# Moving the split normed activations to another byte phase in SBUF

## The chip, the cores and the metric

The kernel runs on one core of a Trainium2 chip. The metric is device time in microseconds of one execution; lower is better. SBUF is the on-chip memory in which the matmul operands lie, 128 partitions wide; an address below is a byte offset within a partition, and its phase is that offset modulo 256.

## The reference

A two-layer encoder trunk, float32, 256 tokens of width 1024. Each layer runs three sub-layers, each on a normed and modulated copy of the residual stream:

```python
n1 = modulate(rms_norm(h, norm_g[l, 0]), sh1, sc1)
h = h + 0.5 * g1[:, None, :] * swiglu(n1, ffn_wg[l, 0], ffn_wu[l, 0], ffn_wd[l, 0])
n2 = modulate(rms_norm(h, norm_g[l, 1]), sh2, sc2)
y = token_mixing(n2, ...)            # two attentions, gates, two output projections
h = h + g2[:, None, :] * y
n3 = modulate(rms_norm(h, norm_g[l, 2]), sh3, sc3)
h = h + 0.5 * g3[:, None, :] * swiglu(n3, ffn_wg[l, 1], ffn_wu[l, 1], ffn_wd[l, 1])
```

`swiglu` is `(silu(x @ w_gate) * (x @ w_up)) @ w_down` with an inner width of 2816. Shift, scale and gate come from a conditioning vector through a further 1024 x 9216 matrix per layer. A final RMS norm closes the stack.

## The kernel before

Every large product is made in three passes over split operands: each float32 operand is kept as a high part and a low part (`nh` and `nl` for the normed activations, `whi` and `wlo` for weights, `hh` and `hl` for the FFN's inner activations), both of type float32r, and `mm3` issues high x high (L84), low weights x high (L85) and high weights x low (L86). A matmul has a stationary operand, which a weight load (LDWEIGHTS, engine PEld) brings into the array, and a moving operand, which streams through it. In the trace's names `out<-moving,stationary`.

The six sub-layers (`SUBS`) run one after another. An FFN sub-layer (`ffn`) goes through eleven slices of 256 inner columns: `gate_up_mm` makes the slice's gate and up banks, 96 matmuls with `nh` or `nl` moving (256 tokens) and 128 weight columns stationary; `gate_up_act` makes `hh` and `hl`; `down_mm` then has `hh` or `hl` stationary and 512 weight columns moving. The first slice after a boundary is made token-major instead (`tok_hi`, `tok_lo`, L465 to L474): there `nh` or `nl` is stationary and the weights move. The mixer uses the token-major form for `pj` and `kv`, the other form for `pt` (`proj_T`) and for the gates `gt` (`gate_mm`); its merge (`yb`) and its output projection (`wo`) use slots of the weight pool on both sides. `gate_bcast` spreads a gate row over all partitions with the all-ones tile `onesr` stationary and `gh`, `gl` moving (L273, L274).

Weights come through one DMA queue (SP) into four raw buffers in the order of `stream`; `pump` takes the next half tile, casts it on ACT (L299), subtracts on DVE (L300), and asks for the next load when a raw buffer is done. The order on every engine is the program's order.

SBUF is laid out by pools, one after another in the order of their declaration (L45 to L47): `wp` (raw buffers of 8192 bytes and 23 slots of 4096), `op` (`nh`, `nl` of 8192 and three each of `hh`, `hl` of 2048), `sb` (everything else). Within a pool tags follow in order of first use. `wp` starts at 128 modulo 256 and all its and `op`'s tiles are multiples of 256 bytes, so weights, normed activations and FFN activations all lie at 128. `sb` starts at 128 too; its first tiles are `cb` (4096 bytes), eight buffers of 2048, `h0` and `h1` (4096 each), `ccol` (32), `abc` (384), `ngc` (192), `ident` (512) and then `onesr`.

`nh` and `nl` are made by `new_nT` (L395), one buffer each, and written by `mod_hi` (L377, ACT) and `mod_lo` (L392, DVE), in the first sub-layer by `mod_k` (L1142, L1145).

Of the kernel before, what the change touches and what calls it, by code (L numbers as in the profile page):

```python
# [13 lines left out]
F32 = mybir.dt.float32  # L14
F32R = mybir.dt.float32r
# [4 lines left out]
P = 128  # L20
D = 1024
S = 256
# [3 lines left out]
NK = D // P  # L26
# [15 lines left out]
def trunk(tc, a):  # L42
    nc = tc.nc
    with (
        tc.tile_pool(name="wp", bufs=1) as wp,  # L45
        tc.tile_pool(name="op", bufs=1) as op,
        tc.tile_pool(name="sb", bufs=1) as sb,  # L47
        tc.tile_pool(name="ps", bufs=1, space=bass.MemoryType.PSUM) as ps,

# [5 lines left out]
        def nm(s):  # L55
            uid[0] += 1
            return f"{s}_{uid[0]}"
# [7 lines left out]
        def b2(name, shape=(P, 512), dt=F32):  # L65
            return sb.tile(list(shape), dt, tag="b2", bufs=NB2, name=nm(name))
# [13 lines left out]
        def const(name, shape, dt=F32):  # L80
            return sb.tile(list(shape), dt, tag=name, bufs=1, name=name)
# [10 lines left out]
                              reason="order")  # L92


        cb = const("cb", [P, D])
        crow = [b2("crow", (1, D // 2)) for _ in range(2)]
        for hf in range(2):
# [13 lines left out]
        for hf in range(2):  # L111
            x = slice(hf * 512, (hf + 1) * 512)
# [280 lines left out]
                                            nh[:, kk, tok].bitcast(F32), op=ALU.subtract)  # L393

        def new_nT():  # L395
            return (op.tile([P, NK, S], F32R, tag="nh", bufs=1, name=nm("nh")),
                    op.tile([P, NK, S], F32R, tag="nl", bufs=1, name=nm("nl")))

        def residual(l, s, t, x, acc):
            g = mods[(l, s)]["g"]  # L400
# [782 lines left out]
        nc.scalar.dma_start(abc, a["ada_b_col"])  # L1183
        nc.scalar.dma_start(ngc, a["norm_g_col"])
        nT = new_nT()
        xsT = [slot("xsT", (P, 4, S)) for _ in range(2)]
        ns = [Norm(t) for t in range(2)]
# [16 lines left out]
        for i, (l, s) in enumerate(SUBS):  # L1204
            nxt = new_nT() if i + 1 < len(SUBS) else None
            if s == 1:
                norm1 = mixer(i, nT, norm1, consts, nxt)
            else:
                norm1, consts = ffn(i, nT, norm1, (lambda *x, nT=nT: first(nT, *x)) if i == 0 else None, nxt)
            nT = nxt  # L1210
# [78 lines left out]
```

## Time and profile before

| | us |
|---|---|
| median of 3 runs | 1146.72 (1146.51 to 1147.17) |
| the profiled execution, its own time | 1147.27 |
| its span, first to last instruction | 1145.5 |
| PE busy | 1122.6 |
| DVE busy | 868.5 |
| ACT busy | 587.7 |

Busy times of an engine are unions of its instructions' intervals. Matmuls are pipelined: the mean duration of one is longer than the step to the next start, so the step is read from start times and not from durations. The page's slices are 1/40 of the span each.

### The profile page before, as it was taken

What the parts mean: (1) busy time and instruction counts of PE and PEld (TensorE: products, weight loads), DVE (VectorE), ACT (ScalarE), POOL (GpSimd) and SP (SyncE); (2) the same over time, 40 slices, a digit from 0 to 9 for tenths busy, and PEclk for the clock granted to TensorE, in tenths of its full rate; (3) what the DMA queues carried; (4) which work ended last, traced back from release to release, by engine and by line L of the source; (5) the groups of instructions that cost most, each with busy time, mean ns of one, the idle gap of its engine ahead of it and who ended that gap; (6) DMA issues with size and microseconds to landing.
All of it is one profiled execution on the core that took longest, in us unless ns stands there. A gap on an engine that the chain in (4) does not pass through costs nothing.

```text
span 1145.5 us, 19136 instructions
## 1 busy us (share of the span) xinstructions
PE 1122.6 (98%) x7774; PEld 1037.2 (91%) x7774; DVE 868.5 (76%) x1334; ACT 587.7 (51%) x911; POOL 43.2 (4%) x52
## 2 busy tenths in 40 slices
PE   5999999999999999999999999999999999999997
PEld 3999999898899899999989999989889988999996
DVE  6996985899867798896489786469986778765543
ACT  4553474557665554445355445435766547544432
POOL 1000000130000000000000000004000100000000
PEclk9999999999999999999999999999999999999999
DMA  9997995368555388988439977543764454866500
GB/s 325 375 339 288 376 337 188 111 240 316 219 182 185 111 315 334 349 331 315 157 118 357 336 299 263 194 169 137 271 218 166 144 207 151 298 263 222 195 31 37
DMA packets 42584, 271.11 MB, mean 237 GB/s; under 512 B 5624, under 2 KB 6392, under 8 KB 12544
## 3 DMA queue, kind: packets, MB, share of 16 engines
q1 hardware_dynamic: 40036, 267.93, 63.7%
q10 hardware_dynamic: 2460, 1.96, 0.6%
q8 instruction: 61, 1.00, 0.3%
q14 instruction: 27, 0.22, 0.1%
HBM read 268.82 MB, written 1.05 MB: 236 GB/s over the span
## 4 chain that ended last, share of the span: by engine, by line
PE 94%; DVE 2%; issue 1%; DMA 1%; ACT 1%; POOL 0%; POOLq 0%; DVEq 0%; ACTq 0%
PE g L86 7%; PE u L86 7%; PE dn L84 7%; PE u L84 7%; PE dn L85 7%; PE u L85 7%; PE g L85 7%; PE g L84 7%; PE dn L86 7%; PE gt L84 3%; PE gt L86 3%; PE gt L85 3%; PE pt L85 1%; PE pt L84 1%; PE yb L84 1%
## 5 line engine op out<-in xcount | busy, mean ns | idle before, releaser
L300 DVE TENSOR_TENSOR wlo<-raw,whi 128x1024 fp32r<-128x1024 f32 x364 | 437.4, 1220 | 155.4 <-PE u L85 93.1
L299 ACT CAST whi<-raw 128x1024 fp32r<-128x1024 f32 x364 | 373.9, 1050 | 226.2 <-PE u L86 87.1
L84 PE MATMUL g<-nh,whi 128*128 128x256 f32 x656 | 186.5, 284 | 3.6 <-ACT nh L1142 3.6
L86 PE MATMUL g<-nl,whi 128*128 128x256 f32 x656 | 186.3, 284 | 1.6 <-DVE nl L1145 1.6
L84 PE MATMUL u<-nh,whi 128*128 128x256 f32 x656 | 186.3, 284 | 0.0
L85 PE MATMUL u<-nh,wlo 128*128 128x256 f32 x656 | 186.2, 284 | 0.0
L86 PE MATMUL u<-nl,whi 128*128 128x256 f32 x656 | 186.1, 284 | 0.0
L85 PE MATMUL g<-nh,wlo 128*128 128x256 f32 x656 | 186.1, 284 | 0.0
L84 PE MATMUL dn<-whi,hh 128*128 128x512 f32 (+1 forms) x358 | 138.7, 387 | 0.0
L85 PE MATMUL dn<-whi,hl 128*128 128x512 f32 (+1 forms) x358 | 138.4, 387 | 0.0
L86 PE MATMUL dn<-wlo,hh 128*128 128x512 f32 (+1 forms) x358 | 138.0, 386 | 0.0
L84 PEld LDWEIGHTS g<-nh,whi 128*128 128x128 f32 x656 | 126.4, 193 | 5.5 <-ACT nh L1142 4.0
L86 PEld LDWEIGHTS g<-nl,whi 128*128 128x128 f32 x656 | 126.2, 192 | 1.9 <-DVE nl L1145 1.9
L85 PEld LDWEIGHTS g<-nh,wlo 128*128 128x128 f32 x656 | 126.3, 193 | 1.3
L84 PEld LDWEIGHTS u<-nh,whi 128*128 128x128 f32 x656 | 126.6, 193 | 0.0
L86 PEld LDWEIGHTS u<-nl,whi 128*128 128x128 f32 x656 | 126.4, 193 | 0.1
L85 PEld LDWEIGHTS u<-nh,wlo 128*128 128x128 f32 x656 | 126.4, 193 | 0.0
L232 DVE CUSTOM_DVE_ANT_0 raw<-raw,cb 128x1024 f32<-128x1024 f32 x96 | 114.6, 1216 | 9.4 <-DMA raw<-in_ada_t_dram 9.4
L505 ACT ACTIVATE sg<-g 128x512 f32<-128x512 f32 x41 | 24.5, 597 | 109.7 <-PE g L86 109.5
L86 PEld LDWEIGHTS dn<-wlo,hh 128*128 128x128 f32 x358 | 67.3, 188 | 13.8
L84 PEld LDWEIGHTS dn<-whi,hh 128*128 128x128 f32 x358 | 67.4, 188 | 12.6
L85 PEld LDWEIGHTS dn<-whi,hl 128*128 128x128 f32 x358 | 67.4, 188 | 12.3
(202 smaller groups left out, 1895.4 us busy)
## 6 DMA issues: line engine op xcount, KB each, us to landing
raw<-in_w_gu_dram SPq DMA_DIRECT2D x79, 1024.0 KB, 5.9
raw<-in_w_d_dram SPq DMA_DIRECT2D x41, 1024.0 KB, 5.9
raw<-in_ada_t_dram SPq DMA_DIRECT2D x40, 1024.0 KB, 6.0
raw<-in_ada_g_dram SPq DMA_DIRECT2D x24, 1024.0 KB, 5.2
raw<-in_w_in_dram SPq DMA_DIRECT2D x16, 1024.0 KB, 4.9
raw<-in_w_gate_dram SPq DMA_DIRECT2D x16, 1024.0 KB, 4.9
raw<-in_w_gu_dram SPq DMA_DIRECT2D x18, 512.0 KB, 6.2
raw<-in_ada_t_dram SPq DMA_DIRECT2D x16, 512.0 KB, 6.9
```

Source lines behind the costliest of these rows:

```text
L84: nc.tensor.matmul(out, Lh, Rh, start=start, stop=False, skip_group_check=True)
L85: nc.tensor.matmul(out, Ll, Rh, start=False, stop=False, skip_group_check=True)
L86: nc.tensor.matmul(out, Lh, Rl, start=False, stop=stop, skip_group_check=True)
L232: queue("dve", nc.vector.tensor_tensor_reduce(r, r, cb, 1.0, 0.0, op0=ALU.mult, op1=ALU.add, accum_out=col[:, k:k + 1]))
L299: queue("act", nc.scalar.copy(hi, r))
L300: queue("dve", nc.vector.tensor_tensor(lo, r, hi.bitcast(F32), op=ALU.subtract))
L505: nc.scalar.activation(sg, g, AF.Silu)
```

## The change

A pool `mv` is declared between `op` and `sb`. Its first tile, `shift`, has 48 floats (192 bytes) per partition and is never used. `nh` and `nl` move from `op` to `mv`, behind it; they are declared flat, of the same size, and used through a view of the old shape. Thereby they start at 128 + 192 = 320, which is 64 modulo 256. The weights' pool and `hh`, `hl` stay at 128. `sb`, which comes after `mv`, starts 192 bytes later than before.

```diff
         tc.tile_pool(name="op", bufs=1) as op,
+        tc.tile_pool(name="mv", bufs=1) as mv_,
         tc.tile_pool(name="sb", bufs=1) as sb,
@@
+        mv_.tile([P, 48], F32, tag="shift", bufs=1, name="shift")
         cb = const("cb", [P, D])
@@
         def new_nT():
-            return (op.tile([P, NK, S], F32R, tag="nh", bufs=1, name=nm("nh")),
-                    op.tile([P, NK, S], F32R, tag="nl", bufs=1, name=nm("nl")))
+            return (mv_.tile([P, NK * S], F32R, tag="nh", bufs=1, name=nm("nh")).rearrange("p (k x) -> p k x", k=NK),
+                    mv_.tile([P, NK * S], F32R, tag="nl", bufs=1, name=nm("nl")).rearrange("p (k x) -> p k x", k=NK))
```

## Rows read from the trace of the kernel before

**Rows 1.** Page, engine totals (busy us, share, instructions) and granted clock by slice.
```profile
span 1145.5 us, 19136 instructions
PE 1122.6 (98%) x7774; PEld 1037.2 (91%) x7774; DVE 868.5 (76%) x1334; ACT 587.7 (51%) x911; POOL 43.2 (4%) x52
...
PEclk9999999999999999999999999999999999999999
```

**Rows 2.** Page, the chain that ended last, by engine.
```profile
PE 94%; DVE 2%; issue 1%; DMA 1%; ACT 1%; POOL 0%; POOLq 0%; DVEq 0%; ACTq 0%
```

**Rows 3.** Waits of PE, the longest: us in total, times, longest us.
```profile
PE nt L366 <- DVE xs L357: 7.9, 4, 6.5
```

**Rows 4.** Matmul groups by line and shape, xcount | busy us, mean ns | idle.
```profile
L84 PE MATMUL g<-nh,whi 128*128 128x256 f32 x656 | 186.5, 284 | 3.6 <-ACT nh L1142 3.6
L86 PE MATMUL u<-nl,whi 128*128 128x256 f32 x656 | 186.1, 284 | 0.0
...
L84 PE MATMUL dn<-whi,hh 128*128 128x512 f32 x346 | 135.3, 391 | 0.0
...
L86 PE MATMUL gt<-nl,whi 128*128 128x256 f32 x256 | 72.4, 283 | 0.0
...
L86 PE MATMUL pt<-nl,whi 128*128 128x256 f32 x128 | 36.4, 284 | 0.0
L465 PE MATMUL pj<-whi,nh 128*128 128x512 f32 x64 | 25.5, 399 | 0.0
...
L465 PE MATMUL gu<-whi,nh 128*128 128x512 f32 x48 | 18.7, 390 | 0.0
...
L793 PE MATMUL sc<-kaT,qaT 64*128 64x256 f32 x96 | 9.6, 300 | 0.1
...
L465 PE MATMUL kv<-whi,nh 128*128 128x256 f32 x32 | 7.9, 285 | 0.0
```

**Rows 5.** Timeline of PE (start us, duration us), a gate/up block's first start and the next.
```profile
104.01 0.28 PE L84 MATMUL g<-nh,whi 128*128 128x256 f32 x1
...
115.52 0.40 PE L84 MATMUL dn<-whi,hh 128*128 128x512 f32 x1
```

**Rows 6.** Timeline of PE, inside a down block and through the gate broadcast behind it.
```profile
152.00 0.39 PE L86 MATMUL dn<-wlo,hh 128*128 128x512 f32 x1
...
154.72 0.39 PE L86 MATMUL dn<-wlo,hh 128*128 128x512 f32 x1
154.95 0.39 PE L273 MATMUL gb<-gh,onesr 128*128 128x512 f32 x1
...
155.88 0.28 PE L84 MATMUL g<-nh,whi 128*128 128x256 f32 x1
```

**Rows 7.** Timeline of PE, from a down block into the next projection.
```profile
213.28 0.39 PE L465 MATMUL pj<-whi,nh 128*128 128x512 f32 x1
...
214.64 0.39 PE L465 MATMUL pj<-whi,nh 128*128 128x512 f32 x1
```

**Rows 8.** Timeline of PE, the merge after a gate broadcast.
```profile
346.48 0.28 PE L84 MATMUL yb<-oaH,whi 128*128 128x256 f32 x1
...
346.83 0.29 PE L84 MATMUL yb<-oaH,whi 128*128 128x256 f32 x1
346.96 0.28 PE L85 MATMUL yb<-oaH,wlo 128*128 128x256 f32 x1
...
357.99 0.40 PE L84 MATMUL wo<-whi,mT 128*128 128x512 f32 x1
```

**Rows 9.** ACT's split line: xcount, duration ns min/median/max, first and last start.
```profile
L299 ACT CAST whi<-raw x364: 1028/1050/1087, 15.2 to 1104.7; 128x1024 fp32r<-128x1024 f32 x182
```

**Rows 10.** Windows: PE, PEld, DVE, ACT, (POOL) busy; clock; DMA; first two: `nh`, `nl` alone.
```profile
0.00:87.00 87.00, 48.13 (x256) 41.87 (x257) 2.74 (x4) 4.37 (x8) 1.00 0.96 347
0.00:87.00 87.00, 36.71 (x128) 25.30 (x128) 2.74 (x4) 1.00 0.96 347
...
412.00:570.00 158.00, 158.00 (x1124) 149.29 (x1123) 122.72 (x144) 71.07 (x83) 0.95 (x1) 1.00 0.82 310
```

## The prediction

> **What bounds the kernel now.** [...] Then the chain of work that ended last [rows 2]: 94% of it is PE, spread over the three matmul lines of `mm3` (L84 to L86), which all stages share. Then who PE waited for [rows 3]: the longest of four items is 7.9 us in all. So the time is the number of matmuls times the step from one start to the next, plus little.
>
> A busy PE is not a PE at its peak, so the step is the next thing to read, from the start times. A gate/up block (8 k x 2 c x 2 banks x 3 = 96 matmuls of 256 moving columns) runs from 104.01 to 115.52 us [rows 5]: 11.51 us / 96 = 119.9 ns. Inside a down block the starts 152.00 and 154.72 are twelve matmuls of 512 columns apart [rows 6]: 2.72 / 12 = 226.7 ns. The difference, 106.8 ns for 256 more columns, is the column rate; both shapes then carry the same remainder, 119.9 - 106.8 = 13.1 ns. [...] This remainder is what the change can touch. It is large: over the 5,088 matmuls counted below, 13.1 ns each is 67 us.
>
> **The change, part by part.** (1) It adds one pool and one 192-byte tile that nobody writes or reads, and it writes the two normed tiles as flat tiles with a view. No instruction, DMA or semaphore wait is added or removed; the regions read and written by each instruction are the same, so the order on every queue stays, SP's and POOL's included. Cost: nothing, with no cover needed.
>
> (2) `nh` and `nl` move from 128 to 64 modulo 256 (128 + 192 = 320). They are the moving operand of gate/up, of the mixer's gates and of the transposed projections, with the weights at 128 as the stationary one. By [rows 4]: six groups of 656 (two are shown), three of 256 `gt`, three of 128 `pt`: 3936 + 768 + 384 = 5,088 matmuls of 256 columns. They are the stationary operand in the token-major products: three groups of 64 `pj` and three of 48 `gu`, 336 matmuls of 512 columns, and 96 `kv` of 256. Together 5,520 of PE's 7,774 [rows 1] get a stationary and a moving operand 64 bytes apart where both lay at the same phase. The 1,038 `dn` matmuls, in three groups (the shown form is 346 of each), and `yb` and `wo` keep equal phases.
>
> (3) The pool `sb` starts 192 bytes later. Its tiles keep their distances to each other; only the 96 narrow score matmuls [rows 4], a key in `sb` against a query in a slot, change phase. At 13.1 ns each that is 1.3 us either way, the bound of the side effect, and I take nothing.
>
> (4) The engines that write and read the moved tiles: the trace has no copy of one kind at two phases with the same operands, so what a phase costs ACT or DVE is bounded by the spread they show over many slots. The 364 casts of L299 take 1028 to 1087 ns [rows 9]. The instructions on `nh` and `nl` lie beside PE's work, which waits 7.9 us at most for anything of one kind [rows 3]. Nothing, within 1 us.
>
> So all hangs on one unknown: the step of a matmul whose two operands lie 64 bytes apart. The trace of before has no such pair in a long run. The bounds:
>
> Faster end: the remainder vanishes, -13.1 ns. Slower end: the nearest row with unequal phases. In `gate_bcast` the stationary `onesr` lies in `sb` behind `ident`, at 224 (128 + 32 + 384 + 192 + 512 bytes of tiles before it, modulo 256, the larger ones being multiples), and the moving `gh` and `gl` at 128. Four of them start at 154.95 and hand over at 155.88 [rows 6]: 0.93 / 4 = 232.5 ns, 5.8 ns more than the down step just before. That this is not the price of merely switching tiles shows at the hand-over from the down block to the next projection, both phases equal: 213.28 to 214.64 is six matmuls at 226.7 ns from the first one on [rows 7].
>
> Value taken: zero. Two readings speak for it. First, the mean step does not care how the streams lie against each other in time. After a gate broadcast the first 96 `yb` matmuls (two calls of `merge`) run unevenly: three starts to 346.83 and the next at 346.96 are 117 and 130 ns apart on average, yet 346.48 to 357.99 is 11.51 us again [rows 8], the same as the even block of [rows 5]. A cost set by where two readers meet in a 256-byte pattern ought to change when one is shifted by some ns against the other. Second, if placement within SBUF mattered by collision, ACT's and DVE's steady traffic at ever different slots should move either PE's step or their own times; the step stays at 119.9 and the casts within some 3% [rows 5, 9]. The broadcast is only four matmuls long, so its 5.8 ns may be the cost of a transient, and it starts 32 bytes off a multiple of 64, where the new place does not.
>
> [...]
>
> **The sum.** The profiled execution took 1147.27 us, 1.8 around its span; the median of the three runs is 1146.72, 0.55 less. Parts 1, 3, 4: 0. Part 2: 5,520 x 0. Forecast: 1146.7, with its own range 1144.5 to 1149 from the 1.3 us and 1 us above.
>
> **Rivals.** A, faster: equal phases are what the remainder is. For it: one and the same number of cycles once per weight load in both shapes, as when a weight load and a moving stream that start at the same phase keep each other up. Against it: the two readings above and the broadcast, which lies apart and is slower. Price: matmuls before 87 us gain nothing, since there the DMA engines are 96% busy at 347 GB/s [rows 10] and loads would end the waits; that is 256 + 128 = 384 of the 5,088. Left: 4,704. All of it gone: 4,704 x 13.1 = 61.6 us, 1085. Half gone, because the streams are a quarter of the pattern apart and not half: 30.8 us, 1116. Later stages can feed that: from 412 to 570 us DVE is busy 122.72 of 158 us, DMA 82% [rows 10], so 5% more demand fits, with some loss. I take 1116 for A.
>
> B, slower: unequal phases cost what the broadcast shows. For it: the only direct row. Place: the gate/up blocks, where nothing covers a longer step, since PE is the chain. Price: 5,520 x 5.8 ns = 32 us, 1179. If only half of it stays once the streams have settled, 1163. It decides from 2.3 us / 5,520 = 0.4 ns a matmul on, a third of a percent of the step.
>
> C: the change does not do what it says, because the allocator rounds the pool's start and the tiles keep one phase. Then 1146.7 too, and the trace after would look as in the likeliest case. I give it 0.02 within that case: 192 is a multiple of 32, as are the smallest tiles that already follow each other in `sb`.
>
> **How the numbers follow.** Same, C included: 0.42. A: 0.33, of which 0.12 below 1100. B: 0.25, of which 0.07 above 1179. Leaving out those two tails, 0.19, the range is 1100 to 1179. Faster, within, or slower by more than 0.2% (2.3 us, about what a measurement of this kernel tells from no change): 0.33, 0.42, 0.25. The likeliest gives the time.
>
> **What would show it.** In the profile of after: the 96 starts of a gate/up block again 11.5 us apart, and down blocks at 226.7 ns (they must stay there in every case, as their phases are kept). A: the gate/up block shrinks to 10.3 to 10.9 us, PE's waits on loads before 87 us grow. B: it grows to about 12 us. Wrong by another way: a new wait on `nh` or `nl` in who PE waited for, or ACT and DVE times on these tiles that differ by more than the spread above.

## The result, and the profile after

The changed kernel takes 1129.02 us, the median of four executions (1128.36 to 1130.47), against 1146.73 us before on the same chip: ratio 0.9847, 95% interval 0.983 to 0.9864, so 17.7 us or 1.5% faster. The profiled execution took 1128.88 us, its span is 1127.1.

The page of the changed kernel (engine totals as busy us, share, instructions; granted clock by slice; chain by engine):

```profile
span 1127.1 us, 19136 instructions
...
PE 1104.9 (98%) x7774; PEld 1019.7 (90%) x7774; DVE 867.4 (77%) x1334; ACT 588.4 (52%) x911; POOL 43.8 (4%) x52
...
PEclk9999999999999999999999999999999999999999
...
PE 91%; DVE 6%; issue 1%; DMA 1%; ACT 1%; POOL 1%; POOLq 0%; DVEq 0%
```

Against [rows 1] the instructions are the same, PE is busy 17.7 us less (1122.6 to 1104.9), and what it idles hardly changes (22.9 and 22.2 us). The chain [rows 2] names DVE for 6% now, but PE lost no time to it: no DVE wait has grown in the list of waits, whose longest item is this (columns: waiter, what it waited for, total us, times, longest us; before [rows 3]):

```profile
PE nt L369 <- DVE xs L360: 6.9, 2, 5.9
```

So the gain lies in the busy time itself, in the step from one matmul to the next. The matmul groups of the changed kernel (line, shape, count, busy us, mean ns), which answer to [rows 4]:

```profile
L85 PE MATMUL g<-nh,whi 128*128 128x256 f32 x656 | 185.0, 282 | 3.7 <-ACT nh L1145 3.7
...
L85 PE MATMUL dn<-whi,hh 128*128 128x512 f32 x346 | 135.1, 390 | 0.0
...
L87 PE MATMUL gt<-nl,whi 128*128 128x256 f32 x256 | 71.1, 278 | 0.0
...
L468 PE MATMUL pj<-whi,nh 128*128 128x512 f32 x64 | 25.6, 399 | 0.0
```

Durations overlap, so they hint only: `g` and `gt` are a little shorter, `dn` and `pj` are not. The start times tell. The timeline of PE after the change (start us, duration us), at the places of [rows 5 to 8]: a gate/up block, the down block behind it, the start of the next gate/up block; the gate broadcast; six steps of the next projection; 96 steps of the merge; a stretch of 85 gate/up matmuls at the end of a mixer:

```profile
101.15 0.28 PE L85 MATMUL g<-nh,whi 128*128 128x256 f32 x1
...
112.46 0.39 PE L85 MATMUL dn<-whi,hh 128*128 128x512 f32 x1
...
117.90 0.28 PE L85 MATMUL g<-nh,whi 128*128 128x256 f32 x1
...
151.40 0.39 PE L276 MATMUL gb<-gh,onesr 128*128 128x512 f32 x1
...
152.33 0.28 PE L85 MATMUL g<-nh,whi 128*128 128x256 f32 x1
...
209.07 0.39 PE L468 MATMUL pj<-whi,nh 128*128 128x512 f32 x1
...
210.44 0.39 PE L468 MATMUL pj<-whi,nh 128*128 128x512 f32 x1
...
339.35 0.28 PE L85 MATMUL yb<-oaH,whi 128*128 128x256 f32 x1
...
350.87 0.40 PE L85 MATMUL wo<-whi,mT 128*128 128x512 f32 x1
...
398.82 0.28 PE L87 MATMUL u<-nl,whi 128*128 128x256 f32 x1
...
408.48 0.27 PE L520 MATMUL tb<-ident,ht 128*128 128x128 f32 x1
```

The gate/up block takes 11.31 us for its 96 matmuls, 117.8 ns each, against 119.9 [rows 5]. The down block takes 5.44 us for 24, 226.7 ns. The broadcast's four steps are 232.5 ns as before [rows 6], the projection's 1.37 / 6 = 228.3 against 226.7 [rows 7], the merge's 120.0, unchanged [rows 8]. And the last stretch, with the same operands as every gate/up block, runs at 9.66 / 85 = 113.6 ns: at the same phases there are two rhythms. The shorter one is not rare: the first block of 384 has it too from 27.8 us on (355 steps at 113.5 ns on average). In the changed kernel every gate/up block that directly follows a down block runs at 117.8 or 117.9; the faster stretches, at 113.5 to 114.6, all follow something else (transposes, a token-major slice, a gate broadcast), though not everything that does is fast.

I summed the steps from each matmul's start to the next over the whole span, by the tile written (us, profiled executions; a wait counts in the step before it):

| tile | columns | before | after | difference |
|---|---|---|---|---|
| `u` and `g` | 256 | 476.9 | 465.4 | -11.5 |
| `gt` (mixer gates) | 256 | 94.5 | 90.7 | -3.8 |
| `pt` (transposed projections) | 256 | 47.8 | 46.0 | -1.8 |
| `dn` | 512 (36 of 1,074: 256) | 241.3 | 240.6 | -0.7 |
| `pj` | 512 | 46.9 | 47.3 | +0.4 |
| `yb`, `wo`, `gu`, `gb`, `sc` together | | 139.1 | 139.0 | -0.1 |

With `kv` (-0.3), the 64 transposes of 128 columns that the trace also calls `pt` (+0.1) and the wait at the start (-0.6; over all runs it takes between 9.4 and 10.7 us) that is the 18.4 us between the two spans.

The casts of the weights (count, duration min/median/max) and the window up to 87 us (busy us of PE, PEld, DVE, ACT, POOL; clock; DMA share; GB/s), after the change:

```profile
L302 ACT CAST whi<-raw x364: 1030/1051/1092, 14.6 to 1086.7; 128x1024 fp32r<-128x1024 f32 x182
...
0.00:87.00 87.00, 73.41 (x499) 67.28 (x499) 76.47 (x112) 45.38 (x62) 3.36 (x11) 1.00 0.97 360
```

The casts are those of [rows 9]. In the first 87 us the queues moved 360 GB/s where they had moved 347 [rows 10], and PE issued 499 matmuls.

### The profile page after: what moved, and what is told of

Same layout as the page of the kernel before. It is cut to its first block, busy times and chain, and to the rows that moved or that the text cites. A ratio compares the mean times of both kernels' runs of the same rounds, so it can differ in the third digit from the quotient of the medians.

```text
span 1127.1 us, 19136 instructions
## 1 busy us (share of the span) xinstructions
PE 1104.9 (98%) x7774; PEld 1019.7 (90%) x7774; DVE 867.4 (77%) x1334; ACT 588.4 (52%) x911; POOL 43.8 (4%) x52
## 4 chain that ended last, share of the span: by engine, by line
PE 91%; DVE 6%; issue 1%; DMA 1%; ACT 1%; POOL 1%; POOLq 0%; DVEq 0%
PE dn L87 7%; PE dn L86 7%; PE dn L85 7%; PE g L87 7%; PE u L85 7%; PE g L85 7%; PE u L87 7%; PE g L86 7%; PE u L86 7%; PE gt L85 3%; PE gt L86 3%; PE gt L87 3%; DVE wlo L303 1%; PE yb L87 1%; PE yb L86 1%; PE yb L85 1%
## 5 line engine op out<-in xcount | busy, mean ns | idle before, releaser
L85 PE MATMUL g<-nh,whi 128*128 128x256 f32 x656 | 185.0, 282 | 3.7 <-ACT nh L1145 3.7
L85 PE MATMUL u<-nh,whi 128*128 128x256 f32 x656 | 184.6, 281 | 0.0
L85 PE MATMUL dn<-whi,hh 128*128 128x512 f32 (+1 forms) x358 | 138.5, 387 | 0.0
L85 PEld LDWEIGHTS g<-nh,whi 128*128 128x128 f32 x656 | 123.8, 189 | 5.5 <-ACT nh L1145 4.1
L86 PEld LDWEIGHTS u<-nh,wlo 128*128 128x128 f32 x656 | 124.1, 189 | 0.0
L85 PEld LDWEIGHTS u<-nh,whi 128*128 128x128 f32 x656 | 123.9, 189 | 0.0
L85 PEld LDWEIGHTS dn<-whi,hh 128*128 128x128 f32 x358 | 67.3, 188 | 12.3
```

What stands on the lines that cost most here:

```text
L85: nc.tensor.matmul(out, Lh, Rh, start=start, stop=False, skip_group_check=True)
L86: nc.tensor.matmul(out, Ll, Rh, start=False, stop=False, skip_group_check=True)
```

## The experiments

Three theories stood at the start. R: the relative phase of the two operands sets the step. K: the place of `nh` and `nl` itself does. S: it is the side effect, `sb` lying 192 bytes further. Two came with the second round. N: only matmuls of 256 columns can gain, and the down step stays at 226.7 ns. L: a block of matmuls falls into one of a few repeating patterns, and the phase decides which. That it also matters how a block is entered was added after that round. Below, d is the phase of the stationary operand less that of the moving one, modulo 256: 0 before, +64 in the gate/up blocks of the changed kernel. Each run is one execution of the kernel named, beside the kernel before on the same chip; the two timed in rounds say so. All keep the whole computation. The rows are PE's timeline: the start of a gate/up block of 96 and the first down matmul behind it, where not said otherwise.

**Half a pattern apart.** `nh` and `nl` at 0, d = 128; against the change:

```diff
-        mv_.tile([P, 48], F32, tag="shift", bufs=1, name="shift")
+        mv_.tile([P, 32], F32, tag="shift", bufs=1, name="shift")
```

> nh and nl at 0 modulo 256, half a pattern from the weights at 128. Theory R (the phase difference of a matmul's two operands sets its step): if the remainder of 13.1 ns falls with the distance, as 64 bytes took it to 117.8 ns in most gate/up blocks and 113.6 in some, 128 bytes take it to 107 to 113 ns everywhere: 1095 to 1115 us. Rival K (64 is a good place for a moving operand, whatever the other's place): the gain is lost or changed without order, 1130 to 1150 us. Rival S (the pool sb moved by 192 bytes and that is what helped): now it moves by 128, no order is expected, near 1129 to 1147 us.

```profile
103.56 0.28 PE L85 MATMUL g<-nh,whi 128*128 128x256 f32 x1
...
115.07 0.39 PE L85 MATMUL dn<-whi,hh 128*128 128x512 f32 x1
```

1145.62 us against 1146.29. The block takes 11.51 us, 119.9 ns. Half a pattern apart is worth next to nothing: the gain does not grow with the distance, and R in the form expected here misses. As `nh` and `nl` lie in `mv` here too, the move to another pool is not the cause either.

**The other direction.** `nh` and `nl` at 192, d = -64: the same line with 16 floats.

> nh and nl at 192 modulo 256: 64 bytes from the weights as in the change, but on the other side. Theory R with the bare distance: the same as the change, 1126 to 1132 us. Theory R with a direction (who leads counts): another time, either back at 1147 or above, up to 1165 us, or lower than the change. Rival K: no gain, 1147 us.

```profile
103.08 0.28 PE L85 MATMUL g<-nh,whi 128*128 128x256 f32 x1
...
114.39 0.40 PE L85 MATMUL dn<-whi,hh 128*128 128x512 f32 x1
```

1137.52 us against 1146.29, half the gain. The block is at 117.8 ns as in the change, but no gate/up block of this kernel reaches 113.6, and `gt` and `pt` gain 1.4 and 0.9 us where the change gave 3.8 and 1.8. None of the cases expected has this time: the direction counts, and what it changes here is mostly which stretches reach the shorter rhythm.

**Everything at 64.** The pools as before, but a 192-byte tile is the first in `wp`, so weights, normed and FFN activations and `sb` all shift together, d = 0:

```diff
+        wp.tile([P, 48], F32, tag="shift", bufs=1, name="shift")
```

> One 192-byte tile ahead of everything: weights, normed and FFN activations and the pool sb all go from 128 to 64 and keep equal phases. Theory R: 1146.7 us, gate/up step 119.9 ns. Rival K: the gain of the change or more, 1115 to 1130 us.

```profile
104.11 0.28 PE L84 MATMUL g<-nh,whi 128*128 128x256 f32 x1
...
115.62 0.40 PE L84 MATMUL dn<-whi,hh 128*128 128x512 f32 x1
```

1147.31 us against 1146.29, and 119.9 ns. `nh` and `nl` lie at 64 as in the change, and nothing is gained. K falls.

**The side effect alone.** The pool `mv` with the 192-byte tile only; `nh` and `nl` stay in `op`, d = 0:

```diff
-            return (mv_.tile([P, NK * S], F32R, tag="nh", ...
-                    mv_.tile([P, NK * S], F32R, tag="nl", ...
+            return (op.tile([P, NK, S], F32R, tag="nh", bufs=1, name=nm("nh")),
+                    op.tile([P, NK, S], F32R, tag="nl", bufs=1, name=nm("nl")))
```

> nh and nl stay at 128, only the pool sb starts 192 bytes later as in the change. Theory R: 1146.7 us within 1.5, gate/up step 119.9 ns. Rival S: 1129 us.

```profile
103.58 0.28 PE L85 MATMUL g<-nh,whi 128*128 128x256 f32 x1
...
115.10 0.40 PE L85 MATMUL dn<-whi,hh 128*128 128x512 f32 x1
```

1146.56 us against 1146.29: S falls. Of the three, R is left: where the two operands lie against each other changes the step, and not the place of one of them. What R does not explain is two rhythms at the same phases.

**The change, and the FFN activations at 192.** `nh`, `nl` stay at 64; now the down blocks have d = +64 too:

```diff
+        op.tile([P, 16], F32, tag="oshift", bufs=1, name="oshift")
-        mv_.tile([P, 48], F32, tag="shift", bufs=1, name="shift")
+        mv_.tile([P, 32], F32, tag="shift", bufs=1, name="shift")
```

> The change, and hh, hl at 192, so that in the down blocks too the stationary operand lies 64 bytes above the moving one. Theory R (phase difference and who leads set the step of any split matmul): the down step falls from 226.7 to between 220 and 224.5 ns, 1,038 matmuls, 2 to 7 us, 1122 to 1127 us. [...]

A down block, the gate/up block behind it, the next down block, and the next gate/up block with its end:

```profile
96.95 0.39 PE L85 MATMUL dn<-whi,hh 128*128 128x512 f32 x1
...
102.53 0.28 PE L85 MATMUL g<-nh,whi 128*128 128x256 f32 x1
...
113.85 0.39 PE L85 MATMUL dn<-whi,hh 128*128 128x512 f32 x1
...
119.45 0.28 PE L85 MATMUL g<-nh,whi 128*128 128x256 f32 x1
...
130.35 0.39 PE L85 MATMUL dn<-whi,hh 128*128 128x512 f32 x1
```

1130.38 us against 1146.92. The down step rose to 5.58 / 24 = 232.5 and 5.60 / 24 = 233.3 ns, over the span +5.4 us against before. The distance that shortens a 256-column step lengthens a 512-column one; neither R's fall nor N's unchanged 226.7 came. And the gate/up blocks, whose phases are those of the change, gave another 4.5 us: the two shown take 11.32 and 10.90 us, 117.9 and 113.5 ns. Of the 27 gate/up blocks that run whole (96 or 192 matmuls), 13 run below 115 ns here, 2 in the changed kernel. The two alternate: wherever only a down block lies between, a block behind one at 113.4 to 114.6 ns runs at 117.8, and a block behind one at 117.8 runs at 113.4 to 113.6. So the phases of a block do not fix its rhythm; what ran before it does its part, which neither R nor L says.

**32 bytes to either side.** `nh`, `nl` at 96, d = +32 (56 floats), and at 32, d = +96 (40 floats).

> nh and nl at 96: 32 bytes below the weights instead of 64. Theory R as a smooth function: a step between 117.8 and 119.9 in the gate/up blocks, 1135 to 1142 us. Theory L (the streams lock into one of a few repeating patterns, with steps of 120.0, 117.8 and 113.4 ns, and the phase only decides which): one of these steps again, so about 1129, 1146 or below 1115 us.

```profile
103.14 0.28 PE L85 MATMUL g<-nh,whi 128*128 128x256 f32 x1
...
114.50 0.40 PE L85 MATMUL dn<-whi,hh 128*128 128x512 f32 x1
```

> nh and nl at 32: 96 bytes below the weights. Theory R as a smooth function: between 117.8 (64 bytes) and 119.9 (128 bytes) in the gate/up blocks, 1135 to 1142 us. Theory L: one of the steps 120.0, 117.8, 113.4 again, so about 1129, 1146 or below 1115 us.

```profile
102.54 0.28 PE L85 MATMUL g<-nh,whi 128*128 128x256 f32 x1
...
113.93 0.39 PE L85 MATMUL dn<-whi,hh 128*128 128x512 f32 x1
```

1140.49 and 1140.05 us against 1146.92; 118.3 and 118.6 ns. The times are those of R as a smooth function. Two steps that the other runs do not have, so L's "a few" is too few. With 128 (1146.7), 96, 64 (1129.0), 32 and 0 (1145.6) the time has one low point among these, at 64.

**One of the two.** `nh` at 64 in `mv`, `nl` back in `op` at 128: two of the three passes of `mm3` have d = +64, the third 0.

```diff
-                    mv_.tile([P, NK * S], F32R, tag="nl", ...
+                    op.tile([P, NK, S], F32R, tag="nl", bufs=1, name=nm("nl")))
```

> Only nh at 64; nl at 128 again, so two of three gate/up matmuls differ in phase and one does not. If each matmul pays by its own phases: two thirds of the gain, gate/up step 118.5 ns, 1134 to 1136 us. If the pattern of the stream as a whole counts (theory L): another step, with anything from no gain (1146) to the whole (1129).

```profile
103.41 0.28 PE L85 MATMUL g<-nh,whi 128*128 128x256 f32 x1
...
114.72 0.39 PE L85 MATMUL dn<-whi,hh 128*128 128x512 f32 x1
```

1138.22 us against 1146.92, half the gain. This block has the 117.8 ns of the change, and so have 25 of the 27 whole blocks, though a third of their matmuls kept d = 0: a matmul does not simply pay by its own phases, which would have given 118.5. None reaches 113.6, some shorter stretches run at 119.3, and `gt` gains 0.9 us of 3.8. For the whole gain both tiles have to move.

**The FFN activations on the other side.** The change with `hh`, `hl` at 64, so d = -64 in the down blocks:

```diff
+        op.tile([P, 48], F32, tag="oshift", bufs=1, name="oshift")
-        mv_.tile([P, 48], F32, tag="shift", bufs=1, name="shift")
```

> The change, and the split FFN activations hh, hl moved as well, to 64 modulo 256, so that in the down blocks the stationary operand lies 64 below the moving weights instead of on their phase; nh, nl stay at 64, so every phase of the gate/up blocks is that of the changed kernel. Where only the distance of the two operands counts and not which is the higher, the down step rises as with the activations at 192 (232.8 ns against 226.7) and the time stands some 5 us worse in the down blocks. Where the direction counts (64 below is not 64 above), the down step is 226.7 ns or less. For the gate/up blocks: if a block's pattern were fixed by its own phases, most blocks run at 117.8 ns and a few at 113.4, as with the change; if it depends on how the block is entered, from a down block with another rhythm, the share of the 113.4 ns blocks changes, as it did with the activations at 192. Time by the first: 1129 us plus or minus the down term (1129 to 1135); by the second: 1120 to 1131.

A down block, two gate/up blocks in a row and the down block behind the second; between the two lie a down block and the gate broadcast:

```profile
129.60 0.39 PE L85 MATMUL dn<-whi,hh 128*128 128x512 f32 x1
...
135.09 0.28 PE L85 MATMUL g<-nh,whi 128*128 128x256 f32 x1
...
146.00 0.39 PE L85 MATMUL dn<-whi,hh 128*128 128x512 f32 x1
...
152.42 0.28 PE L85 MATMUL g<-nh,whi 128*128 128x256 f32 x1
...
163.73 0.40 PE L85 MATMUL dn<-whi,hh 128*128 128x512 f32 x1
...
169.33 0.28 PE L85 MATMUL g<-nh,whi 128*128 128x256 f32 x1
```

In rounds: 1121.65 us, median of four (1120.46 to 1122.41), ratio to before 0.978, 0.9764 to 0.9796. That is 7.4 us below the change, and the intervals do not touch: this version beats both kernels. 25 of the 27 whole gate/up blocks run below 115 ns, and `u` and `g` together lose 21.3 us against before. The two blocks shown have one code and one set of phases: entered from a down block, 10.91 us or 113.6 ns; entered from a down block and the broadcast behind it, 11.31 us or 117.8. A broadcast alone does not decide it, for two shorter stretches behind one, with gate/up matmuls ahead of it, run at 113.6 and 114.2. The pattern is handed on: the down block behind the second takes 5.60 us, 233.3 ns, while those behind blocks at 113.6 are at 229 (the first row to the second, 5.49 us). Direction counts too: behind a block at 113.6, 229 ns at d = -64 against 232.5 at +64. Expected for that case was 226.7 or less.

The down blocks differ from the gate/up blocks in the width and in the roles of the operands: here the activations are stationary. A stretch near the end of this kernel separates the two, 18 `dn` matmuls of 256 columns with the same tiles, roles and d as the 512-column ones beside them. From the first to the next 512-column matmul, in the kernel before (L84) and here (L85):

```profile
1129.99 0.28 PE L84 MATMUL dn<-whi,hh 128*128 128x256 f32 x1
...
1132.14 0.40 PE L84 MATMUL dn<-whi,hh 128*128 128x512 f32 x1
```

```profile
1103.92 0.28 PE L85 MATMUL dn<-whi,hh 128*128 128x256 f32 x1
...
1105.96 0.39 PE L85 MATMUL dn<-whi,hh 128*128 128x512 f32 x1
```

2.15 us or 119.4 ns before, 2.04 us or 113.3 ns here: at one distance and in one role the 256-column matmuls gain and the 512-column ones lose. So it is the width that turns the gain into a loss: of these two widths only the narrower gains, as N has it.

**Between the 32-byte places.** `nh`, `nl` at 80, d = +48, and at 48, d = +80; the tiles still start on multiples of 32 bytes (shift 48 and 40 floats), and the views begin 16 bytes into wider ones:

```diff
-            return (mv_.tile([P, NK * S], F32R, tag="nh", bufs=1, name=nm("nh")).rearrange(...
+            return (mv_.tile([P, NK * S + 64], F32R, tag="nh", bufs=1, name=nm("nh"))[:, 4:NK * S + 4].rearrange(...
```

> The split normed activations nh, nl at 80 modulo 256 (16 bytes further than the change has them), weights and FFN activations at 128 as before. At 96 the kernel took 1140.5 us, at 64 1129.0. Smooth dependence on the relative phase: between the two, 1132 to 1138 us, and a gate/up step between 117.4 and 118.3 ns. A few repeating patterns only, chosen by the phase: the time of either 64 or 96, 1129 or 1140.5. If the 16 bytes matter as such (the operand no longer on a 32-byte step), a longer time than either, above 1141 us.

```profile
103.43 0.28 PE L85 MATMUL g<-nh,whi 128*128 128x256 f32 x1
...
114.87 0.39 PE L85 MATMUL dn<-whi,hh 128*128 128x512 f32 x1
```

> The split normed activations nh, nl at 48 modulo 256 (16 bytes nearer than the change has them), weights and FFN activations at 128 as before. At 32 the kernel took 1140.1 us, at 64 1129.0. Smooth dependence on the relative phase: between the two, 1132 to 1138 us. A few repeating patterns only: 1129 or 1140. If the 16 bytes matter as such, above 1141 us; with the activations at 80 the same sign is then expected.

```profile
103.73 0.28 PE L85 MATMUL g<-nh,whi 128*128 128x256 f32 x1
...
115.17 0.40 PE L85 MATMUL dn<-whi,hh 128*128 128x512 f32 x1
```

1142.7 and 1144.14 us against 1146.89; both blocks 11.44 us, 119.2 ns. Worse than their neighbours on both sides: a smooth curve between the places falls, and both lie above 1141 us, as expected if 16 bytes off a multiple of 32 cost as such.

**The FFN activations at 0.** The change with d = 128 in the down blocks (tiles of 32 and 16 floats in `op` and `mv`).

> The change, with the split FFN activations hh, hl at 0 modulo 256 (half a pattern from the moving weights in the down blocks); nh, nl stay at 64, so the phases of the gate/up blocks are those of the changed kernel. With hh, hl at 128 the share of gate/up blocks at 113.4 to 113.6 ns was small, at 192 about half, at 64 nearly all. Theory that the rhythm of the down block chooses the pattern of the next gate/up block, and that any displaced activation breaks it loose: the larger share of the blocks at 113.6 ns again, down step near 226.7 to 228.5 ns (half a pattern apart cost and gained little in the gate/up blocks), 1117 to 1122 us. Rival, that it needs the stationary operand in the down blocks 64 below: 117.8 ns in most blocks, 1127 to 1131 us. Rival, that the down step is hurt by every distance: 229 ns or more in the down blocks, and 1122 us or longer.

A gate/up block, and the down block behind it up to the next gate/up start:

```profile
119.53 0.28 PE L85 MATMUL g<-nh,whi 128*128 128x256 f32 x1
...
130.42 0.39 PE L85 MATMUL dn<-whi,hh 128*128 128x512 f32 x1
...
135.99 0.28 PE L85 MATMUL g<-nh,whi 128*128 128x256 f32 x1
```

In rounds: 1125.05 us (1124.11 to 1125.91) against 1147.47, ratio 0.9803, 0.9787 to 0.9819. 10.89 us or 113.4 ns for the gate/up block, and 22 of 27 below 115: the larger share comes back, so it does not need the direction of the run before, and that rival falls. But the down step is 5.57 / 24 = 232.1 ns, where I had expected 226.7 to 228.5; the rival by which every distance hurts there had the right number. A distance of 128 is nearly neutral in the gate/up blocks and costs 5.4 ns a matmul in the down blocks.

The steps together (ns; the usual one of whole blocks between 84 and 150 us):

| d | gate/up, 256 columns | down, 512 columns |
|---|---|---|
| 0 | 119.9 | 226.7 to 228.6 |
| +32 | 118.3 | |
| +48 | 119.2 | |
| +64 | 117.8 or 113.4 to 113.6 | 232.5 to 233.3 |
| +80 | 119.2 | |
| +96 | 118.6 | |
| 128 | 119.9 | 232.1 to 232.5 |
| -64 | 117.8 | 229.0, behind a 117.8 block 233.3 |

At d = 0 the second half of a down block runs at 226.7 ns in every kernel (median over the blocks). Its first steps depend on the gate/up block ahead: the whole block takes 226.7 ns a matmul in the change, 227.8 before, and 228.6 with `nh`, `nl` at 96 or 48. That too is handed on. Nor is +64 the only distance with two rhythms: the whole blocks behind a broadcast run at 118.6 at d = 128 and at 117.4 at +96.

## Why the prediction was right or wrong

The time fell into the range of 1100 to 1179, but the likeliest case did not happen. The range spans the prices of all three cases, so that the time lies in it is no merit of the mechanism. What happened comes nearest to rival A, at just over half of its price.

**What bounds the kernel: right.** The span fell by 18.4 us and PE's busy time by 17.7, at nearly unchanged idle time (22.9 and 22.2 us) and the same granted clock (0.998 in both). The number of matmuls times the step is the time.

**The remainder of 13.1 ns, one and the same in both shapes: built in, not found.** Two shapes and two unknowns, a time per column and a remainder, always come out so. The runs speak against it: a distance of 64 takes 2.1 to 6.5 ns off a step of 256 columns and adds 2.3 to 6.6 to one of 512.

**Parts 1, 3 and 4, nothing each: right.** The instructions are the same; the side effect alone gave 1146.56 against 1146.29; the casts take 1030 to 1092 ns, DVE is busy 867.4 us where it was 868.5 and ACT 588.4 where it was 587.7, about the 1 us that was allowed. The spread over many slots was no bound for the cost of a phase, as all slots share one; the runs give it directly: the instructions that write `nh` and `nl` take 462 and 687 ns at the median where they took 460 and 682. Rival C, an allocator that rounds the shift away, falls with the new step.

**"Value taken: zero": this step failed.** Both readings behind it were true as observations, and neither carried the conclusion. The first took two streams that run unevenly in time for two streams shifted in address. The merge, whose operands keep d = 0, still runs at 120.0 ns after the change; yet moving both tiles by 64 bytes takes 2.1 to 6.5 ns off the step of the others. A shift in time at d = 0 was never a test of a shift in address. Nor does the reading hold elsewhere: at d = +64 the mean step is 117.8 or 113.6 by what ran before. The second argued from ACT's and DVE's traffic, beside which the step stayed at 119.9 ns and the casts within some 3% [rows 5, 9], to the place of PE's own two operands, for which it had no row. Besides, the weight slots are 4096 bytes apart, so that all of that traffic lay at one phase. The runs decide: 119.9 ns at d = 0 against 113.6 at +64. They show that the two operands' addresses act on the step together; what in the engine or in the memory does it, no run here shows.

**Rival A: right that the phase holds part of the remainder, wrong in size and reach.** That equal phases are what the remainder is does not hold: at d = 128 the phases differ and the step is 119.9 still, and the 512-column step is shortest at equal phases (226.7 to 228.6 ns). That a weight load and a stream which start at one phase keep each other up was my conjecture; no run shows it. Three terms can be sized. First, the remainder of 13.1 ns. Nearly all gate/up blocks of the change lost 2.1 ns of it (119.9 to 117.8), a few stretches 6.3. The "half gone" that I took for all, 6.5 ns, is the 113.4 to 113.6 ns rhythm; of the 27 whole blocks two come near it (10.97 us, 114.3 ns), and none shows the 10.3 to 10.9 us that I had named as A's sign. In the kernel with `hh`, `hl` at 64 25 of 27 reach it, and it gains 25.2 us by the medians where A had said 30.8. That this would depend on how a block is entered was in no case of mine. Second, the reason given for the half, a quarter of the pattern against half of it: at half of it the gain is gone (1145.62), so nothing like the full price was to be had that way. Third, the 384 matmuls before 87 us, left out because the DMA engines were 96% busy: their steps went from 131.9 to 126.7 ns, 2.0 us, and the first down block starts at 68.07 instead of 70.68. No wait of PE on a load took its place; the queues moved 360 GB/s instead of 347. A busy share of 96% was not a limit here. The shortest stretch shown here is at 113.3 ns a matmul (the 256-column `dn` with `hh`, `hl` at 64), so nowhere did the whole remainder go.

**Rival B: the row was right and did not carry over.** The broadcast's 5.8 ns belongs to matmuls of 512 columns. There it is real: against the change's 226.7 ns the down step rose by 5.4 to 6.6 ns at two of the distances tried and mostly by 2.3 at the third, and the projection pays 228.3 against 226.7 after the change. I laid it on 5,520 matmuls of which only 336 have 512 columns. The row of the other shape was the wrong neighbour, and I had dismissed it as a transient besides.

**The down blocks stay at 226.7: right,** and a little more: behind a 119.9 ns block the 24 took 5.47 us before (115.52 to 120.99), now 5.44; that is most of the 0.7 us.

**The count of 5,520 matmuls: too wide.** `u`, `g`, `gt` and `pt` carry 17.1 of the 18.4 us; the 336 of `pj` and `gu`, of 512 columns with `nh` and `nl` stationary, gain nothing. The 96 of `kv`, with the same roles and 256 columns, gain 0.3.

**Open:** by what a block falls into one rhythm or the other at the same phases; why the wider matmul loses where the narrower one gains; and whether 256 bytes is the period, since the distances tried all lay within it. All but two of the experiments are one execution each.

## What to carry to other kernels

When PE is the chain and its step is longer than the columns explain, the place of the two operands against each other is worth a run: a shift tile costs 192 bytes and moved the time by 1.5 to 2.2% here. Tune it for each matmul shape on its own, by start times over a whole block and not by durations, and look at the blocks behind and before too, since the rhythm is handed on (117.8 or 113.6 ns at the same phases here). Price an unknown with the row nearest in shape, and do not read "insensitive to time" as "insensitive to address". The numbers here are those of one kernel and one type of operand (float32r).

## What the runs showed of the hardware that I had not expected

The step of a 256-column matmul with a new weight load usually took 119.9, 119.2, 118.6, 118.3 or 117.8 ns by nothing but the relative place of its operands in SBUF; shifting both by the same bytes changed nothing (119.9 ns, 1147.31 us). At the same phases a whole block of 96 took 117.8 or 113.6 ns a matmul; with `hh`, `hl` at 192 the two alternate from block to block. In the 512-column blocks every distance tried cost 2.3 to 6.6 ns against 226.7, while 256-column matmuls of the same tiles gained (119.4 to 113.3). Sixteen bytes off a multiple of 32 gave back most of the gain (119.2 ns at +48, between 118.3 at +32 and 117.8 at +64).
